# Log-sum-exp on one core: VectorE's aligned jump moved behind the last row's sum, and the two range checks cut differently

## The chip, the core and the metric

The kernel runs on one core of a Trainium2 chip. A core has five engines that take instructions from their own streams and meet through semaphores: TensorE (PE; its weight loads are shown as PEld), VectorE (DVE), ScalarE (ACT), GpSimd (POOL) and SyncE (SP), which here only issues transfers. Sixteen DMA engines carry the transfers between the device memory and the on-chip memory (SBUF, 128 partitions). The metric is the device time of one execution in microseconds (us), the median of several runs.

## The reference

```python
def setup_inputs():
    batch, seq, dim = 32, 512, 1024
    return {"x": np.random.randn(batch, seq, dim).astype(np.float32)}

def reference(x):
    max_x = np.max(x, axis=-1, keepdims=True)
    return (max_x.squeeze(-1) + np.log(np.sum(np.exp(x - max_x), axis=-1))).astype(np.float32)
```

For each of 16,384 rows of 1,024 numbers the logarithm of the sum of the exponentials is wanted: 67 MB are read and 64 KB written.

## The kernel before

**Fast way and slow way.** The kernel sums exp(x) without taking the maximum off. That is safe as long as every sum lies between `LOW` = 1e-15 and `HIGH` = 1e15. So it checks the sums, brings the verdict into one number (`count`, summed up by TensorE, then `fine` = 1 if it is below `HIGH`), and ScalarE and VectorE read `fine` and branch over a slow way that would compute everything again with the maximum. With this input the slow way is not taken.

**Tiling.** Each of the 128 partitions holds 128 rows, and one column of `sumexp` is the sum of one row per partition. The first `W` = 112 rows of a partition come in nine loads (`LOADS`), the last `B` = 16 rows in nine smaller pieces (`late`). All go through one ring of 48 rows in SBUF. SyncE issues the loads in order and waits only for ring space.

**The first 112 rows.** ScalarE takes the exponential in place (L226). For the operations named `R` VectorE sums whole rows (L237); for those named `F` GpSimd first adds the two halves of each row (L231) and VectorE sums the half rows (L190).

**The last 16 rows.** The pieces are cut across rows: columns 528 to 4288, then 12288 to 15776, then five pieces of 2656, 2000, 1456, 1088 and 800 columns up to column 12288, then the last 608 columns (`BACK`, the end of row 15), and last the first 528 columns (`HEAD`, the start of row 0). ScalarE takes the exponential of a piece (L280), and VectorE sums each row that is complete with an instruction that adds the two halves and accumulates (the helper `halves`, L199). It makes one instruction of the kind SCALAR_TENSOR_TENSOR and one DVE_READ_ACCUMULATOR that writes the column. Rows 0 and 15 are summed in two parts: `parts` holds the sums of the earlier parts; ScalarE writes the logarithm of each part's half, twice, next to the piece that is still to come (L310, tile `joins` in the ring), so that the exponential of the last pieces (L273 for row 15, L265 for row 0) adds the earlier part by its own accumulator. Row 15's sum goes to the last column of `sumexp`, row 0's to `last_sum` in PSUM.

**Checks.** `check_early` clamps `parts` and the 112 finished columns to the range and compares with the values (L159, L164); TensorE multiplies the result into `count` (L169). For each late row `add_up` lets TensorE add its column to `count` (L177), so that a sum too large shows there. A late check (L330) finds columns that are too small, over the 15 columns of rows 1 to 15. A last one (L340) looks at the largest input of the head piece, and TensorE's L345 closes `count`, from which VectorE makes `fine` (L347).

**Order and queues.** Nothing is scheduled by a planner: each engine runs what the code writes for it in that order, and a waiting instruction holds back all that stands behind it on its engine. `Counted.wait` writes a wait for another engine's count only when it is new. ScalarE's last work is the logarithm of 15 columns (L321), then that of row 0 (L323); then SyncE stores the last 16 columns of `res` (L325). The first 112 columns are stored before (L317). At its end SyncE waits for `done` from ScalarE and VectorE and for the early store, clears the semaphores (L406), and waits for the last store (L408).

**The aligned jump.** `addr_align(128, offset=0, max_nops=0)` in VectorE's stream puts the next instruction at the start of a block of 128 instructions; a branch jumps over the unused places. It stands before the sum of the last complete row (row 11, after the 800-column piece):

```python
        if k == len(late) - 3:
            nc.vector.addr_align(128, offset=0, max_nops=0)
        dve.wait(act, at)
```

Of the kernel before, what the change touches and what calls it, by code (L numbers as in the profile page):

```python
# [12 lines left out]
LOW, HIGH = 1e-15, 1e15  # L13
# [3 lines left out]
B = 16  # L17
# [39 lines left out]
def kernel(  # L57
# [5 lines left out]
    nc = tc.nc  # L63
# [4 lines left out]
    P = nc.NUM_PARTITIONS  # L68
    fp32 = mybir.dt.float32
    i32 = mybir.dt.int32  # L70
    AF = mybir.ActivationFunctionType
    AX = mybir.AxisListType
    ALU = mybir.AluOpType

    x_flat = x.flatten_outer_dims()
    n, d = x_flat.shape
    assert n % P == 0
    NC = n // P
    H = d // 2
    W = NC - B  # L80
# [6 lines left out]
    def source(e0, size):  # L87
        assert e0 >= W * d or e0 + size <= W * d
        return x_rest[:, e0 - W * d : e0 - W * d + size] if e0 >= W * d else x_rows[:, e0 : e0 + size]
# [8 lines left out]
    late = [(HEAD, start), (MID * d, B * d - BACK)]  # L98
# [2 lines left out]
        start += size  # L101
    late += [(B * d - BACK, B * d), (0, HEAD)]
    assert start == MID * d and sum(e - s for s, e in late) == B * d

    def sbuf(name, cols, dtype=fp32, rows=P):
        return nc.alloc_sbuf_tensor(name, [rows, cols], dtype).ap()

    ring = sbuf("ring", RING * d)
    sums_all = sbuf("sumexp", 2 + NC)
    parts, sumexp = sums_all[:, 0:2], sums_all[:, 2 : 2 + NC]  # L110
    res = sbuf("res", NC)
    clamped = sbuf("clamped", NC)
    bad = sbuf("bad", 3)
# [11 lines left out]
    act = Counted(nc, nc.scalar, "act")  # L125
    dve = Counted(nc, nc.vector, "dve")
# [16 lines left out]
    def load(i, here, done_before, size):  # L143
        for a, b, who, at in users:
            if a < here + size and b > here:
                sp.wait(who, at)
        users[:] = [u for u in users if not (u[0] < here + size and u[1] > here)]
        parts = [(0, FIRST), (FIRST, size)] if i == 0 else [(0, size)]
        return [
            nc.sync.dma_start(  # L150
                out=ring[:, here + a : here + b], in_=source(done_before + a, b - a)
            ).then_inc(landed[i], 16)
            for a, b in parts
        ]

    def check_early():
        n = 2 + W
        dve.wait(dve, dve.n)
        dve.did(nc.vector.tensor_scalar(  # L159
            out=clamped[:, 0:n], in0=sums_all[:, 0:n],  # L160
            scalar1=LOW, scalar2=HIGH, op0=ALU.max, op1=ALU.min,
        ))
        dve.wait(dve, dve.n)
        dve.did(nc.vector.scalar_tensor_tensor(  # L164
            out=clamped[:, 0:n], in0=clamped[:, 0:n], scalar=0.0, in1=sums_all[:, 0:n],
            op0=ALU.bypass, op1=ALU.not_equal, accum_out=bad[:, 0:1],
        ))
        pe.wait(dve, dve.n)
        pe.did(nc.tensor.matmul(count, lhsT=bad[:, 0:1], rhs=far, start=True, stop=False))  # L169
# [3 lines left out]
    def add_up():  # L173
        while sums:
            c, who, at = sums.pop(0)
            pe.wait(who, at)
            pe.did(nc.tensor.matmul(  # L177
                count, lhsT=ones, rhs=sumexp[:, c : c + 1], start=False, stop=False
            ))
# [3 lines left out]
    def reduce_folded():  # L183

        nonlocal early_sum
        while folded:
            c0, s0, p0, n0 = folded.pop(0)
            halves = ring[:, p0 : p0 + s0 * d].rearrange("p (c d) -> p c d", d=d)[:, :, 0:H]
            dve.wait(pool, n0)
            at = dve.did(nc.vector.reduce_sum(  # L190
                out=sumexp[:, c0 : c0 + s0], in_=halves, axis=AX.X
            ))
            users.append((p0, p0 + s0 * d, dve, at))
            if c0 < W:
                early_sum = at

    def halves(v, c):
        n = v.shape[1] // 2
        return dve.did(nc.vector.scalar_tensor_tensor(  # L199
            out=v[:, 0:n], in0=v[:, 0:n], scalar=1.0, in1=v[:, n : 2 * n],  # L200
            op0=ALU.mult, op1=ALU.add, accum_out=c,
        ))

    c = 0
# [5 lines left out]
    for i, (size, ops) in enumerate(loads):  # L210
# [11 lines left out]
        for k, (how, s) in enumerate(ops):  # L222
# [5 lines left out]
            if how == "F":  # L228
# [3 lines left out]
                    out=rows[:, :, 0:H], in0=rows[:, :, 0:H], in1=rows[:, :, H:d], op=ALU.add  # L232
# [15 lines left out]
    def place(e0):  # L248
        return e0 - MID * d + p if e0 >= MID * d else gap + GAP + e0

    joins = bass.AP(
        tensor=ring.tensor, offset=ring[:, gap : gap + 1].offset,
        ap=[ring.ap[0], [GAP - 2, 2], [1, 2]],
    )
    summed = set()
    seen = []
    for k, (s, e) in enumerate(late):
        i = len(loads) + k
        at0, at1 = place(s), place(s) + e - s
        [dma] = load(i, at0, W * d + s, e - s)  # L260
        act.wait(landed[i], 16)
        if k >= len(late) - 2:
            act.wait(act, joined)
        if k == len(late) - 1:
            head_sum = act.did(nc.scalar.activation(  # L265
                out=last_exp[:, 0 : e - s + 2], in_=ring[:, at0 - 2 : at1], func=AF.Exp,
                accum_out=last_sum,
            ))
            break
        if k == len(late) - 2:  # L270
            assert at1 == gap
            v = ring[:, at0 : at1 + 2]
            back_sum = act.did(nc.scalar.activation(  # L273
                out=v, in_=v, func=AF.Exp, accum_out=sumexp[:, NC - 1 : NC]
            ))
            sums.append((NC - 1, act, back_sum))
            add_up()
            continue
        v = ring[:, at0:at1]
        at = act.did(nc.scalar.activation(out=v, in_=v, func=AF.Exp))  # L280
        if k == 0:
            reduce_folded()
        if k == len(late) - 3:
            nc.vector.addr_align(128, offset=0, max_nops=0)
        dve.wait(act, at)
        seen.append((s, e))
        for r in range(1, B - 1):
            left = r * d
            for s0, e0 in sorted(seen):
                if s0 <= left < e0:  # L290
                    left = e0
            if r not in summed and left >= (r + 1) * d:
                summed.add(r)
                row = ring[:, place(r * d) : place(r * d) + d]
                sums.append((W + r, dve, halves(row, sumexp[:, W + r : W + r + 1])))
        if k == 0:
            halves(ring[:, at0 : place(0) + d], parts[:, 1:2])
        if k == 1:
            halves(ring[:, place((B - 1) * d) : at1], parts[:, 0:1])
            both = dve.n  # L300
            act.wait(dve, early_sum)
            ln_early = act.did(nc.scalar.activation(  # L302
                out=res[:, 0:W], in_=sumexp[:, 0:W], func=AF.Ln
            ))
            check_early()
        if k >= 1:
            add_up()
        if k == 2:
            act.wait(dve, both)
            joined = act.did(nc.scalar.activation(  # L310
                out=joins, in_=parts[:, :, None].to_broadcast([P, 2, 2]), func=AF.Ln, scale=0.5
            ))
    assert len(summed) == B - 2

# [1 line left out]
    sp.wait(landed[-2], 16)  # L316
    nc.sync.dma_start(out=out_rows, in_=res[:, 0:W]).then_inc(sp.sem, 16)  # L317

    act.wait(dve, dve.n)
    act.wait(act, back_sum)  # L320
    act.did(nc.scalar.activation(out=res[:, W + 1 : NC], in_=sumexp[:, W + 1 : NC], func=AF.Ln))  # L321
    act.wait(act, head_sum)
    act.did(nc.scalar.activation(out=res[:, W : W + 1], in_=last_sum, func=AF.Ln))  # L323
    sp.wait(act, act.n)
    nc.sync.dma_start(out=out_rest, in_=res[:, W:NC]).then_inc(stored, 16)  # L325


    dve.wait(dve, dve.n)
    dve.wait(act, back_sum)
    dve.did(nc.vector.scalar_tensor_tensor(  # L330
        out=clamped[:, W + 1 : NC], in0=sumexp[:, W + 1 : NC], scalar=LOW,
        in1=sumexp[:, W + 1 : NC], op0=ALU.max, op1=ALU.not_equal, accum_out=bad[:, 1:2],
    ))
    pe.wait(dve, dve.n)
    pe.did(nc.tensor.matmul(count, lhsT=bad[:, 1:2], rhs=far, start=False, stop=False))
    pe.wait(dve, less_at)
# [4 lines left out]
        out=over, in0=ring[:, at0 : at0 + half], scalar=CEILING,  # L341
        in1=ring[:, at0 + half : at1], op0=ALU.max, op1=ALU.max, accum_out=bad[:, 2:3],
# [15 lines left out]
    with nc.If(all_fine < 1):  # L358
# [5 lines left out]
        for c0 in range(0, NC, RING):  # L364
# [6 lines left out]
            for c1, c2 in ((c0, edge), (edge, c0 + s)):  # L371
                if c1 == c2:
                    continue
                nc.scalar.dma_start(
                    out=ring[:, (c1 - c0) * d : (c2 - c0) * d],
                    in_=source(c1 * d, (c2 - c1) * d),
# [4 lines left out]
                out=neg, in_=v, op=ALU.max, axis=AX.X, negate=True  # L381
# [3 lines left out]
                out=v, in0=v, in1=neg[:, :, None].to_broadcast([P, s, d])  # L385
# [5 lines left out]
                out=sumexp[:, c0 : c0 + s], in_=v, axis=AX.X  # L391
# [71 lines left out]
```

## Time and profile before

| what | value |
|---|---|
| median of 3 runs | 161.93 us (161.88 to 162.07) |
| profiled execution | 161.83 us |
| its span, first to last instruction | 160.1 us |
| VectorE busy | 114.2 us (71%) |
| ScalarE busy | 114.5 us (71%) |
| TensorE busy | 2.5 us (2%) |
| GpSimd busy | 37.3 us (23%) |
| mean transfer rate over the span | 420 GB/s |

The span is 1.7 us shorter than the execution's time; what lies around the span is not in the program. The busy shares are means over the whole span: the engines wait for loads early on, and are full only in the last 15 us. The chain of work that ended last is followed back by the profile from the last busy instruction; branches, semaphore instructions and the landing of a store are not busy work, so the chain does not hold what comes after 158.98 us.

### The profile page before, as it was taken

The page shows a single profiled execution, that of the slowest core. Times are in us where ns is not written, and L with a number is a line of the kernel's source. Part 1 is how long each engine was busy: PE and PEld are TensorE (multiplying, and loading weights), DVE is VectorE, ACT ScalarE, POOL GpSimd, SP SyncE. Part 2 cuts the span into 40 slices and gives each one's busy share as a digit, 9 for nine tenths or more (in the row PEclk, how much of TensorE's full clock was granted, in tenths as well). Part 3 has the DMA queues.
Part 4 walks back from the last instruction along what each step waited for, and adds up shares of the span by engine and source line. Part 5 has one row for each costly group of instructions (what it writes and reads, how often), then busy time and mean ns, then how long its engine had stood idle before and what let it go on. Part 6 is the DMA issues. An engine that isn't in the chain of part 4 may idle for free.

```text
span 160.1 us, 250 instructions
## 1 busy us (share of the span) xinstructions
PE 2.5 (2%) x38; PEld 1.3 (1%) x38; DVE 114.2 (71%) x60; ACT 114.5 (71%) x32; POOL 37.3 (23%) x11
## 2 busy tenths in 40 slices
PE   0000000000000000000000000000000000000033
PEld 0000000000000000000000000000000000000011
DVE  0000000019999499994999859959999999999986
ACT  3000059980799709995099949992999989799996
POOL 0000000000000000000000993690004979891000
DMA  8995996996996996997999999999999999999993
GB/s 319 507 507 254 507 524 262 524 524 262 524 524 262 524 524 262 524 475 311 483 442 442 442 426 409 409 409 472 405 396 454 458 409 393 421 437 425 414 402 114
DMA packets 3025, 67.18 MB, mean 420 GB/s; under 512 B 592, under 2 KB 592, under 8 KB 1488
## 3 DMA queue, kind: packets, MB, share of 16 engines
q1 hardware_dynamic: 3024, 67.18, 97.8%
q14 instruction: 1, 0.01, 0.0%
HBM read 67.11 MB, written 0.07 MB: 419 GB/s over the span
## 4 chain that ended last, share of the span: by engine, by line
DMA 51%; ACT 27%; DVE 20%; issue 0%; PE 0%
DMA ring<-in_x_dram 51%; ACT ring L226 19%; DVE sumexp L237 16%; ACT ring L280 7%; DVE sumexp L190 2%; DVE ring L199 2%; DVE over L340 0%; PE count L345 0%; ACT res L302 0%; DVE clamped L330 0%; DVE fine L347 0%; ACT ring L310 0%
## 5 line engine op out<-in xcount | busy, mean ns | idle before, releaser
L226 ACT ACTIVATE ring<-ring 128x16384 f32<-128x16384 f32 (+9 forms) x16 | 98.0, 6169 | 42.3 <-DMA ring<-in_x_dram 42.3
L237 DVE TENSOR_REDUCE sumexp<-ring 128x16 f32<-128x16384 f32 (+4 forms) x9 | 85.6, 9514 | 42.0 <-ACT ring L226 42.0
L231 POOL TENSOR_TENSOR ring<-ring 128x3072 f32<-128x3072 f32 (+3 forms) x7 | 37.1, 5314 | 107.1 <-ACT ring L226 107.1
L190 DVE TENSOR_REDUCE sumexp<-ring 128x6 f32<-128x3072 f32 (+3 forms) x7 | 18.4, 2659 | 0.0
L280 ACT ACTIVATE ring<-ring 128x3760 f32<-128x3760 f32 (+6 forms) x7 | 13.7, 2006 | 0.0
L199 DVE SCALAR_TENSOR_TENSOR ring<-ring 128x512 f32<-128x512 f32 (+2 forms) x16 | 9.6, 652 | 0.4 <-ACT ring L280 0.3
L135 ACT ACT_TABLE_LOAD x1 | 1.3, 1283 | 1.9 <-PEq L66 1.9
L169 PE MATMUL count<-far,bad 128*1 128x1 f32 x2 | 0.2, 164 | 152.6 <-DVE clamped L164 152.6
L177 PE MATMUL count<-sumexp,ones 128*1 128x1 f32 x30 | 2.0, 163 | 3.6 <-DVE ring L199 3.5
L136 DVE MEMSET ones<- 128x1 f32 x1 | 0.1, 59 | 2.0 <-PEq L66 2.0
L169 PEld LDWEIGHTS count<-far,bad 128*1 128x1 f32 x2 | 0.1, 82 | 152.6 <-DVE clamped L164 152.6
L199 DVE DVE_READ_ACCUMULATOR ring<-ring 128x1 f32 x16 | 1.4, 85 | 0.0
L177 PEld LDWEIGHTS count<-sumexp,ones 128*1 128x1 f32 x30 | 1.1, 81 | 4.5 <-DVE ring L199 4.5
L273 ACT ACTIVATE ring<-ring 128x610 f32<-128x610 f32 x1 | 0.7, 696 | 0.0
L265 ACT ACTIVATE last_exp<-ring 128x530 f32<-128x530 f32 x1 | 0.6, 595 | 0.0
L340 DVE SCALAR_TENSOR_TENSOR over<-ring 128x264 f32<-128x264 f32 x1 | 0.4, 428 | 0.0
L347 DVE TENSOR_SCALAR fine<-count 1x1 int32<-1x1 f32 x1 | 0.1, 146 | 0.3 <-PE count L345 0.3
L164 DVE SCALAR_TENSOR_TENSOR clamped<-clamped,sumexp 128x114 f32<-128x114 f32 x1 | 0.3, 279 | 0.0
L302 ACT ACTIVATE res<-sumexp 128x112 f32<-128x112 f32 x1 | 0.3, 278 | 0.0
L159 DVE TENSOR_SCALAR clamped<-sumexp 128x114 f32<-128x114 f32 x1 | 0.2, 221 | 0.0
L321 ACT ACTIVATE res<-sumexp 128x15 f32<-128x15 f32 x1 | 0.2, 203 | 0.0
L330 DVE SCALAR_TENSOR_TENSOR clamped<-sumexp 128x15 f32<-128x15 f32 x1 | 0.2, 174 | 0.0
(20 smaller groups left out, 2.3 us busy)
## 6 DMA issues: line engine op xcount, KB each, us to landing
ring<-in_x_dram SPq DMA_DIRECT2D x1, 7936.0 KB, 21.2
ring<-in_x_dram SPq DMA_DIRECT2D x1, 6912.0 KB, 23.9
ring<-in_x_dram SPq DMA_DIRECT2D x1, 6400.0 KB, 19.7
ring<-in_x_dram SPq DMA_DIRECT2D x1, 4608.0 KB, 15.9
ring<-in_x_dram SPq DMA_DIRECT2D x1, 3584.0 KB, 24.0
ring<-in_x_dram SPq DMA_DIRECT2D x1, 3072.0 KB, 19.1
ring<-in_x_dram SPq DMA_DIRECT2D x1, 1880.0 KB, 16.0
ring<-in_x_dram SPq DMA_DIRECT2D x1, 1744.0 KB, 19.8
```

The costliest lines, as they stand in the source:

```text
L135: nc.scalar.preload_act_table_set("natural_log_exp_and_others")
L169: pe.did(nc.tensor.matmul(count, lhsT=bad[:, 0:1], rhs=far, start=True, stop=False))
L177: pe.did(nc.tensor.matmul(count, lhsT=ones, rhs=sumexp[:, c : c + 1], start=False, stop=False))
L190: at = dve.did(nc.vector.reduce_sum(out=sumexp[:, c0 : c0 + s0], in_=halves, axis=AX.X))
L199: return dve.did(nc.vector.scalar_tensor_tensor(out=v[:, 0:n], in0=v[:, 0:n], scalar=1.0, in1=v[:, n : 2 * n], op0=ALU.mult, op1=ALU.add, ...
L226: at = act.did(nc.scalar.activation(out=v, in_=v, func=AF.Exp))
L231: at = pool.did(nc.gpsimd.tensor_tensor(out=rows[:, :, 0:H], in0=rows[:, :, 0:H], in1=rows[:, :, H:d], op=ALU.add))
L237: at = dve.did(nc.vector.reduce_sum(out=sumexp[:, c : c + s], in_=rows, axis=AX.X))
L265: head_sum = act.did(nc.scalar.activation(out=last_exp[:, 0 : e - s + 2], in_=ring[:, at0 - 2 : at1], func=AF.Exp, accum_out=last_sum,))
L273: back_sum = act.did(nc.scalar.activation(out=v, in_=v, func=AF.Exp, accum_out=sumexp[:, NC - 1 : NC]))
L280: at = act.did(nc.scalar.activation(out=v, in_=v, func=AF.Exp))
L340: dve.did(nc.vector.scalar_tensor_tensor(out=over, in0=ring[:, at0 : at0 + half], scalar=CEILING, in1=ring[:, at0 + half : at1], op0=ALU.m ...
```

## The change

Three things change. The sum of the first part of row 0 moves into `sumexp`'s own column of row 0, and the part of row 15 stands just ahead of the first column, so that one stretch of 1 + 112 + 4 = 117 columns holds both parts, the 112 early sums and the late rows 1 to 3. The early check runs over these 117 columns instead of 114; the late check over 12 columns (rows 4 to 15) instead of 15, and TensorE no longer adds the columns of rows 1 to 3 (`c < LATE`). The aligned jump moves from before the last row's sum to behind it. The late check is written ahead of ScalarE's late logarithm, which then waits for the check's count alone; it waited for the last row's sum and for row 15's sum.

```diff
+    LATE = W + late[0][1] // d
...
-    sums_all = sbuf("sumexp", 2 + NC)
-    parts, sumexp = sums_all[:, 0:2], sums_all[:, 2 : 2 + NC]
+    sums_all = sbuf("sumexp", 1 + NC)
+    sumexp = sums_all[:, 1 : 1 + NC]
+    part_15, part_0 = sums_all[:, 0:1], sumexp[:, W : W + 1]
+    parts = bass.AP(
+        tensor=sums_all.tensor, offset=sums_all.offset,
+        ap=[sums_all.ap[0], [1 + W, 2], [0, 2]],
+    )
...
     def check_early():
-        n = 2 + W
+        n = 1 + LATE
...
             c, who, at = sums.pop(0)
+            if c < LATE:
+                continue
...
-        if k == len(late) - 3:
-            nc.vector.addr_align(128, offset=0, max_nops=0)
         dve.wait(act, at)
...
+    nc.vector.addr_align(128, offset=0, max_nops=0)
+    dve.wait(dve, dve.n)
+    dve.wait(act, back_sum)
+    dve.did(nc.vector.scalar_tensor_tensor(
+        out=clamped[:, LATE:NC], in0=sumexp[:, LATE:NC], scalar=LOW,
+        in1=sumexp[:, LATE:NC], op0=ALU.max, op1=ALU.not_equal, accum_out=bad[:, 1:2],
+    ))
     act.wait(dve, dve.n)
-    act.wait(act, back_sum)
     act.did(nc.scalar.activation(out=res[:, W + 1 : NC], in_=sumexp[:, W + 1 : NC], func=AF.Ln))
     act.wait(act, head_sum)
...
-    dve.wait(dve, dve.n)
-    dve.wait(act, back_sum)
-    dve.did(nc.vector.scalar_tensor_tensor(
-        out=clamped[:, W + 1 : NC], in0=sumexp[:, W + 1 : NC], scalar=LOW,
-        in1=sumexp[:, W + 1 : NC], op0=ALU.max, op1=ALU.not_equal, accum_out=bad[:, 1:2],
-    ))
```

In the built program this is VectorE's end, by source line, operation, tiles (written, then read) and the semaphores that it waits for (`act`, `dve`, `pe` are counts of ScalarE, VectorE and TensorE; `landed17` is the last load's). ISA is the aligned jump. First before, then after:

```order
L199 SCALAR_TENSOR_TENSOR ring,sumexp<-ring 128x512
L199 SCALAR_TENSOR_TENSOR ring,sumexp<-ring 128x512 [waits act]
L284 ISA
L199 SCALAR_TENSOR_TENSOR ring,sumexp<-ring 128x512 [waits act]
L330 SCALAR_TENSOR_TENSOR clamped,bad<-sumexp 128x15 [waits act,dve]
L340 SCALAR_TENSOR_TENSOR over,bad<-ring 128x264 [waits landed17]
L347 TENSOR_SCALAR fine<-count 1x1 [waits pe]
```

And the same place after the change:

```order
L208 SCALAR_TENSOR_TENSOR ring,sumexp<-ring 128x512
L208 SCALAR_TENSOR_TENSOR ring,sumexp<-ring 128x512 [waits act] x2
L326 ISA
L329 SCALAR_TENSOR_TENSOR clamped,bad<-sumexp 128x12 [waits act,dve]
L346 SCALAR_TENSOR_TENSOR over,bad<-ring 128x264 [waits landed17]
L353 TENSOR_SCALAR fine<-count 1x1 [waits pe]
```

The jump has moved past one row's sum and now stands right ahead of the late check; the check itself and what follows keep their places and waits.

ScalarE's end before, from the last two plain exponentials to the reading of `fine`:

```order
L280 ACTIVATE ring<-ring 128x800 [waits landed15]
L273 ACTIVATE ring,sumexp<-ring 128x610 [waits act,landed16]
L265 ACTIVATE last_exp,last_sum<-ring 128x530 [waits landed17]
L321 ACTIVATE res<-sumexp 128x15 [waits act,dve]
L323 ACTIVATE res<-last_sum 128x1 [waits act]
L351 TENSOR_LOAD fine [waits dve]
```

And after:

```order
L289 ACTIVATE ring<-ring 128x800 [waits landed15]
L282 ACTIVATE ring,sumexp<-ring 128x610 [waits act,landed16]
L274 ACTIVATE last_exp,last_sum<-ring 128x530 [waits landed17]
L334 ACTIVATE res<-sumexp 128x15 [waits dve]
L336 ACTIVATE res<-last_sum 128x1 [waits act]
L357 TENSOR_LOAD fine [waits dve]
```

The order is the same; the late logarithm has one wait fewer, and the VectorE count it waits for is one instruction later, the late check's.

TensorE's stream before, whole:

```order
L458 UNCONDITIONAL_BRANCH [waits barrier_Pool_Activation_PE_DVE_SP_release]
L169 MATMUL count<-far,bad 1x1 [waits barrier_Pool_Activation_PE_DVE_SP_release,dve]
L177 MATMUL count<-sumexp,ones 1x1 x6
L177 MATMUL count<-sumexp,ones 1x1 [waits dve] x8
L177 MATMUL count<-sumexp,ones 1x1 [waits act]
L335 MATMUL count<-far,bad 1x1 [waits dve]
L337 MATMUL count<-steep,less 1x1
L345 MATMUL count<-steep,bad 1x1 [waits dve]
```

And after:

```order
L464 UNCONDITIONAL_BRANCH [waits barrier_Pool_Activation_PE_DVE_SP_release]
L176 MATMUL count<-far,bad 1x1 [waits barrier_Pool_Activation_PE_DVE_SP_release,dve]
L186 MATMUL count<-sumexp,ones 1x1 x3
L186 MATMUL count<-sumexp,ones 1x1 [waits dve] x8
L186 MATMUL count<-sumexp,ones 1x1 [waits act]
L341 MATMUL count<-far,bad 1x1 [waits dve]
L343 MATMUL count<-steep,less 1x1
L351 MATMUL count<-steep,bad 1x1 [waits dve]
```

Three column sums, those of rows 1 to 3, are gone from the stretch that needs no new wait.

More of the change, by code (lines that the diff above doesn't have):

```diff
@@ L296 @@
         if k == 0:
-            halves(ring[:, at0 : place(0) + d], parts[:, 1:2])
+            halves(ring[:, at0 : place(0) + d], part_0)
         if k == 1:
-            halves(ring[:, place((B - 1) * d) : at1], parts[:, 0:1])
+            halves(ring[:, place((B - 1) * d) : at1], part_15)
             both = dve.n
@@ L310 @@
             joined = act.did(nc.scalar.activation(
-                out=joins, in_=parts[:, :, None].to_broadcast([P, 2, 2]), func=AF.Ln, scale=0.5
+                out=joins, in_=parts, func=AF.Ln, scale=0.5
             ))
```

## The prediction

> **What bounds the kernel now.** I read the chain of work that ended last, then the order of time over the last 10 us, then what SyncE waited for, and last the DMA queues in short stretches of the end. The change touches nothing before the early check at 152 us, so only the end is worked through. The chain's last links (start, us, what):
>
> ```profile
> core 0 of [0], span 160.1 us
> ...
> 152.29 3.12 ACT ring L280 x2
> 155.42 0.02 issue
> 155.44 1.10 DVE ring L199 x3
> 156.54 0.13 issue
> 156.67 1.32 DVE ring L199 x5
> 157.99 0.02 issue
> 158.01 0.18 DVE clamped L330 x2
> ...
> 158.83 0.15 DVE fine L347
> ```
>
> By this chain VectorE's row sums would set the end. But it stops with the last busy instruction at 158.98, and the span runs to 160.1. The rows in order of time (start, us, engine, line) show a second chain beside it:
>
> ```profile
> 156.06 0.69 DVE L199 SCALAR_TENSOR_TENSOR ring<-ring 128x512 f32<-128x512 f32 x1
> ...
> 156.67 0.69 DVE L199 SCALAR_TENSOR_TENSOR ring<-ring 128x512 f32<-128x512 f32 x1
> ...
> 157.11 0.70 ACT L273 ACTIVATE ring<-ring 128x610 f32<-128x610 f32 x1
> ...
> 157.28 0.69 DVE L199 SCALAR_TENSOR_TENSOR ring<-ring 128x512 f32<-128x512 f32 x1
> ...
> 157.71 0.19 ACT L273 ACTIVATION_READ_ACCUMULATOR ring<-ring 128x1 f32 x1
> 157.81 0.59 ACT L265 ACTIVATE last_exp<-ring 128x530 f32<-128x530 f32 x1
> 157.90 0.08 DVE L199 DVE_READ_ACCUMULATOR ring<-ring 128x1 f32 x1
> 158.01 0.17 DVE L330 SCALAR_TENSOR_TENSOR clamped<-sumexp 128x15 f32<-128x15 f32 x1
> ...
> 158.12 0.08 DVE L330 DVE_READ_ACCUMULATOR clamped<-sumexp 128x1 f32 x1
> ...
> 158.39 0.20 ACT L321 ACTIVATE res<-sumexp 128x15 f32<-128x15 f32 x1
> ...
> 158.50 0.17 ACT L323 ACTIVATE res<-last_sum 128x1 f32<-128x1 f32 x1
> ...
> 158.69 0.34 SPq L325 DMA_DIRECT2D out_dram<-res  x1
> ```
>
> ScalarE goes without a gap through L273, L265, the late logarithm L321 (it starts at 158.39, as L265 ends at 157.81 + 0.59 = 158.40) and L323, and 0.02 us after that SyncE issues the last store. SyncE's own waits, and the stores' times from issue to landing (KB, us), tell which of the two chains is last:
>
> ```profile
> SPq L406 <- ACTq L403: 0.7, 1, 0.7
> ...
> SPq L408 <- SPq L408: 0.4, 1, 0.4
> ```
> ```profile
> out_dram<-res SPq DMA_DIRECT2D x1, 56.0 KB, 1.9
> ...
> out_dram<-res SPq DMA_DIRECT2D x1, 8.0 KB, 1.4
> ```
>
> L406 is released by the branches behind `fine`; after it SyncE waits 0.4 us more at L408, for the last store: 158.69 + 1.4 = 160.1, the end of the span. So the end is set by ScalarE and the store, and VectorE's check and verdict have about 0.4 us to spare.
>
> **The change part by part.** The sum goes against the profiled execution: span 160.1 plus 1.7 around it, 161.83, which is 0.1 below the median of 161.93.
>
> *Early check, 117 columns for 114.* The neighbours:
>
> ```profile
> 151.99 0.22 DVE L159 TENSOR_SCALAR clamped<-sumexp 128x114 f32<-128x114 f32 x1
> ...
> 152.25 0.28 DVE L164 SCALAR_TENSOR_TENSOR clamped<-clamped,sumexp 128x114 f32<-128x114 f32 x1
> ...
> 152.64 0.75 PE L177 MATMUL count<-sumexp,ones 128*1 128x1 f32 x14
> 153.06 0.08 DVE L199 DVE_READ_ACCUMULATOR ring<-ring 128x1 f32 x1
> ...
> 153.20 0.09 PEld L177 LDWEIGHTS count<-sumexp,ones 128*1 128x1 f32 x2 [0.23 <-DVE ring L199]
> ...
> 154.08 0.69 DVE L199 SCALAR_TENSOR_TENSOR ring<-ring 128x512 f32<-128x512 f32 x1 [0.33 <-ACT ring L280]
> ```
>
> From L164 (114 columns, 0.28) to L330 (15 columns, 0.17) a column costs 0.11 / 99 = 0.0011 us; three more on two instructions are 0.007 us. VectorE then stands idle for 0.33 us before 154.08, waiting for ScalarE: cost nothing, and 0.007 if that cover were gone. The late check gets three columns shorter, 0.003 us less. The part sums only change their place, with the same instructions and sizes; ScalarE's join reads them by another stride, which I put at nothing, since 4 columns go through it either way.
>
> *Three column sums fewer on TensorE.* They are six of the fourteen matmul rows in 0.75 us, so at most 0.3 us at 152.6, after which TensorE waits for VectorE anyway (0.23 at 153.20). No gain on the path.
>
> *The jump.* Its row before:
>
> ```profile
> L284 DVEq COMPARE_BRANCH  x1: 51/51/51, 156.5 to 156.5; - x1
> ```
>
> It ran at 156.5 for 51 ns on VectorE's sequencer while the engine was busy with the sum of 156.06. The sum behind it started at 157.28, 0.61 after its predecessor, as that did after the one of 156.06: the jump cost nothing. From its end (156.55) to 157.28 is 0.73, so with all that it loads it takes less than 0.73 us. After the change it can run when the last row's sum has been sent off, that is when ScalarE's 800 columns are done, 0.09 after 157.11, say at 157.25. Even 0.73 more is 157.98, and the check could not start before 158.01, since it waits for the last row's sum. Bounds for the check's delay: 0 and 0.02 (a branch that is sent one 51 ns step later); I take 0, nearest to the row of 157.28.
>
> *The late logarithm's wait.* The check is done at 158.12 + 0.08 = 158.20. From VectorE's accumulator read at 153.06 + 0.08 to TensorE's start at 153.20 it took 0.06 to pass a count on, so ScalarE could start at 158.26. It is not free until 158.39: 0.13 to spare. Queued behind the wait are L323, SyncE's store and ScalarE's reading of `fine`; all keep their times as long as that margin holds. The two delays above (0.02 and 0.007) do not use it up. The wait that goes was passed while L265 ran:
>
> ```profile
> L53 ACTq EVENT_SEMAPHORE  x2: 17/17/17, 156.3 to 157.9; - x2
> ```
>
> The second of these, 17 ns at 157.9, is the one removed: it lies within L265 (157.81 to 158.40), a gain between 0 and 0.017, and I take 0. What stays late next is L265 itself, behind the last loads.
>
> *A fetch of instructions beside the stores.* The queues from 157.30 to 157.95, in 40 slices of 0.016 us:
>
> ```profile
> DMA  0000000000000000000000900000000000000000
> GB/s 0 0 0 0 0 0 0 0 0 0 0 0 0 0 0 0 0 0 0 0 0 0 504 0 0 0 0 0 0 0 0 0 0 0 0 0 0 0 0 0
> ...
> q14 instruction: 1, 0.01, 5.1%
> ```
>
> One packet of instructions, the only one in the span, starts in slice 22, at 157.66, and takes 5.1% of 16 engines over 0.65 us, 0.53 us on one engine. If VectorE's jump asks for it (1.11 us earlier), it moves by as much as the jump, 0.75 us, to 158.4 to 158.95. The last store's packets come later:
>
> ```profile
> 158.41:159.50 1.09, 0.27 (x6) 0.09 (x2) 0.29 (x3) 0.26 (x3) 0.00 (x0) 1.00 0.00 0
> 159.53:159.75 0.22, 0.00 (x0) 0.00 (x0) 0.00 (x0) 0.00 (x0) 0.00 (x0) 1.00 0.42 37
> ```
>
> The DMA share (the last number but one) is zero from 158.41 to 159.50 and 0.42 from 159.53: the moved packet falls into an empty stretch. Cost 0; the bound above is in the first rival.
>
> *Sum:* -0.02 to +0.03, taken as 0: profiled about 161.83, median 161.93.
>
> *A rule and a row.* The Trainium skill, page "Runtime: NRT & Kernel Launch", section "Instruction fetch mechanics", says that a taken branch to a page which is not held stalls the engine until a transfer has brought that page. It speaks against this change, since the branch now stands right ahead of the check. The trace disagrees for the jump as it stands: the sum behind it ran at 157.28, ahead of the packet of 157.66. That page of the Trainium skill also has blocks of 16 KiB; 504 GB/s over 0.01625 us are 8 KB here. By the rule the sum would be the second rival's.
>
> **The rivals.**
>
> *First, slower: the packet meets the last store.* It decides if the packet starts after 159.0 (159.53 less 0.53). That would be so if TensorE's stream asks for it and not the jump: TensorE does one column sum every 0.61 us there, and with three fewer it reaches the same place in its stream 1.84 us later, so the packet would start at 157.66 + 1.84 = 159.50. For it speaks only that both engines were at work at 156.5. Against it: 1.11 us after the jump fits a request made there. Price: the 56 KB store, which had the packet beside it, took 1.9 to land, the 8 KB one 1.4, so up to 0.5; at 0.33 it is past the bound. 162.25 to 162.45.
>
> *Second, slower: the jump must wait for its block.* Two more places of the stream now stand ahead of the jump (the sum and its accumulator read). If that moves the next aligned place one block on, that block isn't held: asked for at 157.25, it starts to come 1.11 later and takes 0.53, 158.9. Then check (0.17 + 0.08) and 0.06: the logarithm at 159.2 for 158.39, 0.8 late; past 0.13 every microsecond goes to the end. 162.7.
>
> *Third, faster.* If the packet or the early jump held up the last loads or ScalarE in runs without a profile, moving it gives that back. The profile speaks against it: from 157.11 ScalarE has no gap at all, and the DMA slices are empty from 157.30 until the packet starts, so the loads' packets were through. To count, 0.33 would have to be found in a tail where I find 0.02. 161.5.
>
> **How the numbers follow.** 0.2% of 161.93 is 0.32 us, about what a measurement of this kernel can tell from no change: 161.61 to 162.25. No change on the path: 0.70, with its own range 161.8 to 162.1 by the spread of the runs before (161.88 to 162.07) and the terms' bounds. First rival 0.10, second 0.06, slower for a reason that I don't see 0.04: slower 0.20. Third rival with what I don't see: faster 0.10. The range of 161.65 to 162.35 holds the first case, the lower half of the first rival's price and the weaker form of the third.
>
> **What would show it.** Right: in the profile after, the branch at about 157.25, the late check at 158.01, the late logarithm L334 straight behind L274 at 158.4, the last store 0.3 later and landed after 1.4; the instruction packet 0.7 to 0.8 later than before, in the gap between the two stores. Wrong: ScalarE idle before L334 with VectorE named as the releaser; a late check that starts well after the last row's sum; an instruction packet within the last store, and that store's landing above 1.4; or a second instruction packet in the span.

## The result and the profile after

The changed kernel takes 161.71 us (median of 22 runs, 161.62 to 161.87), the kernel before, in as many runs beside it, 161.99 us (161.72 to 162.33). The ratio is 0.9985, with a 95% interval of 0.9979 to 0.9991: faster by 0.15%, a quarter of a microsecond (the two medians lie 0.28 us apart). That is inside the predicted range and inside the 0.2% which the prediction took for unmeasurable, but 22 runs a side do tell it from nothing, so "no change" was wrong.

The profiled execution after has a span of 160.3 us, no shorter than before. Its chain of work, last links (start, us, what):

```profile
core 0 of [0], span 160.3 us
...
152.43 3.14 ACT ring L289 x2
155.57 0.02 issue
155.60 2.55 DVE ring L208 x8
158.15 0.03 issue
158.18 0.18 DVE clamped L329 x2
...
158.99 0.15 DVE fine L353
```

All of it is 0.16 us later than before, from loads that landed later in this execution. Within the end, in order of time (start, us, engine, line):

```profile
157.28 0.70 ACT L282 ACTIVATE ring<-ring 128x610 f32<-128x610 f32 x1
...
157.97 0.59 ACT L274 ACTIVATE last_exp<-ring 128x530 f32<-128x530 f32 x1
158.05 0.08 DVE L208 DVE_READ_ACCUMULATOR ring<-ring 128x1 f32 x1
158.18 0.17 DVE L329 SCALAR_TENSOR_TENSOR clamped<-sumexp 128x12 f32<-128x12 f32 x1
...
158.56 0.20 ACT L334 ACTIVATE res<-sumexp 128x15 f32<-128x15 f32 x1
...
158.66 0.17 ACT L336 ACTIVATE res<-last_sum 128x1 f32<-128x1 f32 x1
...
158.85 0.34 SPq L338 DMA_DIRECT2D out_dram<-res  x1
```

Counted from the start of row 15's exponential (157.11 before, 157.28 after), the check starts at 0.90 both times, the late logarithm at 1.28, the last store at 1.58 before and 1.57 after. SyncE's last waits and the stores' landing:

```profile
SPq L412 <- ACTq L409: 0.7, 1, 0.7
...
SPq L414 <- SPq L414: 0.4, 1, 0.4
```
```profile
out_dram<-res SPq DMA_DIRECT2D x1, 56.0 KB, 1.6
...
out_dram<-res SPq DMA_DIRECT2D x1, 8.0 KB, 1.4
```

The aligned jump's row after, and the transfers from 158.30 to 159.50 in 40 slices of 0.03 us:

```profile
L326 DVEq COMPARE_BRANCH  x1: 51/51/51, 157.4 to 157.4; - x1
```
```profile
GB/s 299 225 209 135 90 15 0 0 0 273 0 0 0 0 0 0 0 0 0 0 0 0 0 0 0 0 0 0 0 0 0 0 0 0 0 0 0 0 0 0
...
q14 instruction: 1, 0.01, 2.0%
```

The packet of instructions is now in slice 9, at 158.57: behind the early store's data and ahead of the last store's.

So the profile after shows the end that the prediction described, and no gain in it. The gain is in a number that is in no row: an execution's time less its span. For the profiled executions it is 161.83 - 160.14 = 1.69 us before and 161.87 - 160.30 = 1.57 after; over all 22 runs after it is 1.49 on average, with a mean span of 160.23. I call it the part outside the span. The experiments give it for the kernel before too: 1.69 to 1.70 us on average over 21 to 33 runs a time, with a mean span of 160.20 to 160.23. Against these the span has not moved, and the part outside is 0.21 us shorter. The 22 runs of the kernel before that stand beside the change have no spans on record; whether the rest of the 0.28 us between the two medians is more than scatter is not shown.

### The profile page after: what moved, and what is told of

Same layout as the page of the kernel before. It is cut to its first block, busy times and chain, and to the rows that moved or that the text cites. A ratio compares the mean times of both kernels' runs of the same rounds, so it can differ in the third digit from the quotient of the medians.

```text
span 160.3 us, 237 instructions
## 1 busy us (share of the span) xinstructions
PE 2.3 (1%) x32; PEld 1.2 (1%) x32; DVE 114.2 (71%) x60; ACT 114.5 (71%) x32; POOL 37.3 (23%) x11
## 4 chain that ended last, share of the span: by engine, by line
DMA 51%; ACT 27%; DVE 20%; issue 0%; PE 0%
DMA ring<-in_x_dram 51%; ACT ring L235 19%; DVE sumexp L246 16%; ACT ring L289 7%; DVE sumexp L199 2%; DVE ring L208 2%; DVE over L346 0%; PE count L351 0%; ACT res L309 0%; DVE clamped L329 0%; DVE fine L353 0%; ACT ring L317 0%
## 5 line engine op out<-in xcount | busy, mean ns | idle before, releaser
L274 ACT ACTIVATE last_exp<-ring 128x530 f32<-128x530 f32 x1 | 0.6, 593 | 0.0
```

Source lines behind the costliest of these rows:

```text
L274: head_sum = act.did(nc.scalar.activation(out=last_exp[:, 0 : e - s + 2], in_=ring[:, at0 - 2 : at1], func=AF.Exp, accum_out=last_sum,))
```

## The experiments

Each time stands beside runs of the kernel before on the same chip; "outside" is the mean over a kernel's runs of its time less its span (one run scatters by 0.02 to 0.05 us, and spans are on record to 0.1 us). The ratio is that to the kernel before in the same set of runs; in the row "after" that one had 161.99 us. e4 has five runs, the others ten or more. Instructions of ScalarE are counted in the built program, against the kernel before.

| run | what | ScalarE's instructions | median us | ratio, 95% interval | mean span | outside |
|---|---|---|---|---|---|---|
| before | | 0 | 161.90 to 161.92 | | 160.2 | 1.69 to 1.70 |
| after | the change | -1 | 161.71 | 0.9985 [0.9979, 0.9991] | 160.23 | 1.49 |
| e1 | jump alone | 0 | 161.92 | 1.0004 [0.9995, 1.0013] | 160.23 | 1.71 |
| e2 | wait alone | -1 | 161.76 | 0.9988 [0.9979, 0.9997] | 160.20 | 1.54 |
| e3 | columns alone | 0 | 161.89 | 1.0005 [0.9996, 1.0014] | 160.22 | 1.72 |
| e4 | no jump | 0 | 162.42 | 1.0036 [1.0022, 1.005] | 160.76 | 1.70 |
| e5 | after, one more that runs | 0 | 161.85 | 0.9998 [0.9988, 1.0008] | 160.19 | 1.73 |
| e6 | before, one less, not run | -1 | 161.71 | 0.9987 [0.9978, 0.9997] | 160.22 | 1.50 |
| e7 | after, one more, not run | 0 | 161.86 | 0.9998 [0.9988, 1.0007] | 160.18 | 1.70 |
| e8 | after, one less, not run | -2 | 161.51 | 0.9973 [0.9964, 0.9983] | 160.19 | 1.32 |
| e9 | after, two less | -3 | 161.53 | 0.998 [0.9971, 0.9989] | 160.26 | 1.34 |
| e10 | after, many less, not run | -10 | 161.61 | 0.9979 [0.9969, 0.9988] | 160.25 | 1.35 |
| e11 | before, one more, not run | +1 | 161.74 | 0.9988 [0.9979, 0.9997] | 160.20 | 1.53 |
| e12 | before, four more, not run | +4 | 161.83 | 0.9995 [0.9986, 1.0005] | 160.29 | 1.52 |
| e13 | after, ScalarE aligned early | jump | 161.97 | 1.0 [0.9991, 1.0009] | 160.63 | 1.34 |
| e14 | e13, one more, not run | jump | 161.97 | 1.0005 [0.9996, 1.0014] | 160.67 | 1.33 |
| e15 | before, ScalarE aligned early | jump | 161.87 | 0.9998 [0.9989, 1.0008] | 160.62 | 1.34 |
| e16 | after, ScalarE aligned late | jump | 161.56 | 0.9979 [0.997, 0.9988] | 160.19 | 1.37 |
| e17 | before, ScalarE aligned late | jump | 161.59 | 0.9982 [0.9972, 0.9991] | 160.31 | 1.35 |

### The parts one by one: e1, e2, e3

The jump alone:

```diff
-        if k == len(late) - 3:
-            nc.vector.addr_align(128, offset=0, max_nops=0)
...
+    nc.vector.addr_align(128, offset=0, max_nops=0)
     dve.wait(dve, dve.n)
     dve.wait(act, back_sum)
```

> Only the aligned jump is moved behind the last row's sum; checks, waits and column layout are those of the kernel before. Theory A (the jump and its instruction packet held something up in many executions, outside what one profile shows): this kernel alone gives most of the gain, 0.2 to 0.28 us less than before, and its instruction packet starts 0.7 to 0.9 us later, near 158.5. Theory B (the shorter TensorE and ScalarE streams, or the wait, give the gain): within 0.08 us of before. Theory C (the prediction: nothing on the path): also within 0.08 us of before.

The wait alone (the late check, over its old 15 columns, is written ahead of the logarithm):

```diff
+    dve.wait(dve, dve.n)
+    dve.wait(act, back_sum)
+    dve.did(nc.vector.scalar_tensor_tensor(
+        out=clamped[:, W + 1 : NC], in0=sumexp[:, W + 1 : NC], scalar=LOW,
+        in1=sumexp[:, W + 1 : NC], op0=ALU.max, op1=ALU.not_equal, accum_out=bad[:, 1:2],
+    ))
     act.wait(dve, dve.n)
-    act.wait(act, back_sum)
```

> Only the late check is written ahead of the late logarithm, which then waits for the check's count alone; jump and columns as before. Theory A: no gain, within 0.08 us of before. Theory B in the form that ScalarE's removed wait gives it: 0.15 us or more less than before. The prediction: within 0.02 us, the logarithm starting straight behind row 0's exponential.

The columns alone are the change's diff without its two other parts: 117 and 12 columns, three TensorE sums fewer.

> Only the columns are recut: early check over 117 columns, late check over 12, three TensorE column sums fewer; jump and wait as before. Theory A: no gain, within 0.08 us of before. Theory B in the form that TensorE's shorter stream gives it: 0.15 to 0.28 us less than before, and in the part outside the span (1.7 us before, 1.5 after).

The wait alone gives the gain (161.76, 1.54 outside); jump and columns give none (161.92 and 161.89). The instruction packet of e1, in 40 slices of 0.016 us from 158.20 to 158.85:

```profile
GB/s 303 248 303 222 221 221 165 166 83 83 0 28 0 0 0 0 0 0 0 504 0 0 0 0 0 0 0 0 0 0 0 0 0 0 0 0 0 0 0 0
...
q14 instruction: 1, 0.01, 3.7%
```

It starts in slice 19, at 158.51. That of e3, from 157.30 to 157.95:

```profile
GB/s 0 0 0 0 0 0 0 0 0 0 0 0 0 0 0 0 0 0 0 0 0 0 0 504 0 0 0 0 0 0 0 0 0 0 0 0 0 0 0 0
...
q14 instruction: 1, 0.01, 4.5%
```

Slice 23, 157.67, as before the change, although TensorE's stream is three sums shorter here. So the packet follows VectorE's jump and not TensorE.

### No jump at all: e4

```diff
-        if k == len(late) - 3:
-            nc.vector.addr_align(128, offset=0, max_nops=0)
```

> The kernel before without any aligned jump. Theory A: if the jump's place is what costs, taking it away changes the time by 0.2 us or more, faster if the packet alone was the harm, slower if VectorE then crosses into its next block at a worse place. The profile shows whether the instruction packet at 157.7 is the jump's: without the jump it should be gone from the span or start elsewhere; if it stays at 157.7 it is another engine's. Theory B: within 0.08 us of before, packet unmoved if it is TensorE's.

Slower by 0.36%, and this time in the span. In order of time:

```profile
158.03 0.17 DVE L328 SCALAR_TENSOR_TENSOR clamped<-sumexp 128x15 f32<-128x15 f32 x1
...
158.49 0.08 DVE L328 DVE_READ_ACCUMULATOR clamped<-sumexp 128x1 f32 x1 [0.29 <-issue]
...
158.71 0.34 SPq L323 DMA_DIRECT2D out_dram<-res  x1
```

Its transfers from 158.50 to 160.90, in 40 slices of 0.06 us, and the last store's landing:

```profile
GB/s 0 0 0 0 0 0 0 0 0 0 0 0 0 0 0 137 0 19 54 41 18 5 0 0 0 0 0 0 0 0 0 0 0 0 0 0 0 0 0 0
...
q14 instruction: 1, 0.01, 0.8%
```
```profile
out_dram<-res SPq DMA_DIRECT2D x1, 8.0 KB, 2.1
```

Between the check and its own accumulator read, which begins 0.1 us after the check in all the other profiles, VectorE stands for 0.29 us for nothing that the profile shows. I read this as the edge of VectorE's instruction block. Then the packet starts in slice 15 (159.4), just ahead of the last store's data, and that store takes 2.1 us to land instead of 1.4: 158.71 + 2.1 = 160.8, the end of the span. This is the first rival's price, 0.7 us in the profile and 0.5 in the medians. That the packet is the cause is inferred: the store's data rows end at 159.8, hardly later than before, and what keeps the landing back after that is in no row. The early store speaks for it. It lands after 1.9 to 2.1 us in the seven profiles in which VectorE's jump stands ahead of the last row's sum and ScalarE has no late jump, so that the packet comes ahead of the store's data, and after 1.6 us in the nine in which VectorE's jump stands behind that sum and the packet comes later. VectorE's standstill makes the verdict late too: SyncE begins its last wait at about 160.2 here and at 159.7 before, so by these figures the standstill alone would have cost about 0.1 us. If it is the edge of a block, only the check stands between it and the jump of the changed kernel.

### The length of ScalarE's stream: e5 to e8

The wait that the change removes is one instruction of ScalarE, 17 ns within L265's time. e2 cuts nothing else, so either the wait itself or the length of the stream is at work. e5 keeps the new wait and puts one instruction back, far ahead:

```diff
+        if i == 3:
+            nc.scalar.wait_ge(landed[0], 16)
         act.wait(landed[i], 16 * len(dma))
```

> The changed kernel with one instruction more in ScalarE's stream, far from the end: a second wait, long satisfied, ahead of an exponential at about 75 us, so that ScalarE's stream is as long as before the change, while the late logarithm still waits for the check alone. Theory L (the length of ScalarE's stream sets 0.2 us of the part outside the span): time back at that of before, 161.9, and 1.7 us outside the span. Theory S (what the late logarithm waits for gives the gain): as the changed kernel, 161.7, and 1.5 us outside the span. Both: span as before within 0.1.

e6 shortens ScalarE's stream in the kernel before by an instruction of the slow way, which is not taken, and puts it on VectorE (e8 does the same to the changed kernel):

```diff
     with nc.If(all_fine < 1):
-        nc.scalar.wait_ge(sp.sem, 16)
+        nc.vector.wait_ge(sp.sem, 16)
         nc.scalar.wait_ge(stored, 16)
```

> The kernel before, with ScalarE's stream shortened by one instruction that never runs: in the slow way, which this input does not take, the wait for the early store stands on VectorE instead of ScalarE. Nothing that runs is changed. Theory L: 0.15 to 0.25 us faster than before, 1.5 us outside the span. Theory S: as before, 161.9, 1.7 us outside.

e7 lengthens the changed kernel there:

```diff
     with nc.If(all_fine < 1):
+        nc.scalar.wait_ge(landed[0], 16)
+        nc.scalar.wait_ge(landed[1], 16)
         nc.scalar.wait_ge(sp.sem, 16)
```

> The changed kernel with ScalarE's stream lengthened by one instruction that never runs (a second wait in the slow way). Theory L: the gain is gone, 161.9 and 1.7 us outside the span. Theory S: 161.7 and 1.5 us outside. If e5 loses the gain and this keeps it, it is the number of instructions that run, not the length of the stream.

> The changed kernel with ScalarE's stream one instruction shorter still, by the same move in the slow way as in the run on the kernel before. Theory L as a step (an end of a block of instructions that the stream passes or not): no more to gain, 161.7 and 1.5 us outside. Theory L as a slope (each instruction costs): another 0.2 us, 161.5 and 1.3 us outside. Theory S: 161.7.

Theory L holds in all four. One more instruction of ScalarE, run or not, takes the gain away (1.73 and 1.70 outside); one less, never run, gives it to the kernel before (1.50), and a second one gives the changed kernel as much again (1.32, 161.51 us). What the logarithm waits for has no part in it. Nor do the lengths of other streams show one: e6, with one VectorE instruction more, has 1.50 where e2, without it, has 1.54; e3, with three of TensorE fewer, has 1.72; e4, with one of VectorE fewer, 1.70. e5 and e7 change ScalarE's stream alone. e8 looked like a slope of 0.19 us per instruction.

### How far it goes: e9 to e12

e9 is e8 with ScalarE's share of the program's end moved:

```diff
-        if read.ins.engine == mybir.EngineType.DVE:
+        if read.ins.engine == mybir.EngineType.Activation:
             read.then_inc(done, 1)
...
-        nc.scalar.wait_ge(again, rows + 32)
+        nc.vector.wait_ge(again, rows + 32)
...
-    nc.scalar.sem_inc(done, 1)
+    nc.vector.sem_inc(done, 1)
```

> The changed kernel with ScalarE's stream two instructions shorter, by moving work to VectorE and nothing else: the wait for the early store in the slow way, and the signal that ends the program (ScalarE gives its part of it with its reading of the verdict, VectorE at its end). Three fewer than before the change in all. If each instruction of ScalarE's stream costs 0.19 us outside the span, as the last four runs suggest: 1.70 - 3 x 0.19 = 1.13 us outside, 161.33 in all. If the gain ends after two: 1.32 outside, 161.5. Span 160.2 in both.

(In e9 VectorE's stream is two instructions longer than before, in e10 four shorter.) e10 is e9 with `for c0 in range(0, RING, RING)` in the slow way and without its two stores:

> As the run with two fewer, and the slow way, which does not run, is cut to its first third, and its two stores and the last third's loads are left out with it: ten ScalarE instructions fewer than before the change. Shows where the gain ends. On a slope without end: 1.70 - 10 x 0.19 is below zero, so it must end; if it ends at an edge close by, 1.0 to 1.3 us outside and 161.2 to 161.5 in all. If moving an edge brings a new one, the time can also rise.

e11 and e12 are the kernel before with two and with eight waits more in the slow way, which make one and four instructions:

> The kernel before with one ScalarE instruction more that never runs. On the slope: 1.89 us outside the span, 162.1. If the kernel before already stands at the top of the step: 1.70 and 161.9.

> The kernel before with four ScalarE instructions more that never run. On the slope: 1.70 + 4 x 0.19 = 2.46 us outside, 162.7. At the top of a step: 1.70 and 161.9, as with one more.

The slope fell: 1.35, 1.34, 1.32, 1.49 to 1.54, 1.70 to 1.73, 1.53, 1.52 us for -10, -3, -2, -1, 0, +1 and +4 instructions. It is a step with a peak, and the kernel before stood on the peak: one instruction more (e11, of ScalarE alone) would have helped it nearly as much as one less (161.74 and 161.71). In e12 a second packet of instructions is to be seen, behind the span. From 160.30 to 162.00, in slices of 0.043 us:

```profile
GB/s 0 0 0 0 0 0 0 0 0 0 0 0 0 0 0 0 0 0 0 0 0 0 0 0 0 0 0 0 0 0 193 0 0 0 0 0 0 0 0 0
...
q14 instruction: 1, 0.01, 1.7%
```

In the profile before, the same stretch of time holds no packet at all, and no other profile has one behind its span, not even e11's, with one instruction more. So this packet does not mark the peak: e12, which has it, stands at 1.52, and the kernel before, which has none, at 1.70.

### An aligned jump for ScalarE: e13 to e17

If an edge of an instruction block lies among what ScalarE runs behind the program, a jump to the start of a block takes the length out of it.

```diff
+        if i == 3:
+            nc.scalar.addr_align(128, offset=0, max_nops=0)
         act.wait(landed[i], 16 * len(dma))
```

> The changed kernel with an aligned jump in ScalarE's stream too, ahead of the exponential of the fourth load (about 70 us), so that everything behind it, to the end of the program and past it, stands at a set place in a block. Theory E (what costs is an edge of a block that falls on ScalarE's instructions behind the end of the program; the kernel before has its length at the worst place): 1.35 us outside the span or less, 161.5 to 161.6. Theory G (any change of the length shifts the part outside by chance, no edge): no reason for less than the changed kernel's 1.49. Against both: a jump that itself costs would lengthen the span beyond 160.2.

> As the run with ScalarE's aligned jump, and one ScalarE instruction more that never runs, the one that took the whole gain from the changed kernel (1.49 to 1.70 us outside). Theory E: no edge is near any more, so the part outside is the same within 0.05 us of the run without it. Theory G: it moves by 0.1 to 0.2 us.

> The kernel before with ScalarE's aligned jump alone, ahead of the fourth load's exponential; its two waits before the late logarithm stay. Theory E: the same part outside as the changed kernel with that jump, within 0.05 us, so the change's whole gain and more is had without the change. Theory G: 1.5 to 1.7 us outside.

The figures are those of theory E: 1.34, 1.33 and 1.34 us outside. That they come from an edge, and that it lies behind the program, they do not show. The instruction that cost 0.21 us without the jump costs nothing with it, and the kernel before comes to the same figure as the changed one. But the span grew by 0.4 us. The chain of work of e13, and below it of the kernel before, at the same load:

```profile
72.24 24.43 DMA ring<-in_x_dram
```
```profile
72.19 23.87 DMA ring<-in_x_dram
```

The load on which the chain stands took 0.56 us longer. It took 24.38 to 24.59 us in the three runs with this jump and 23.87 to 23.91 in the sixteen others. ScalarE's jump ran at 60.5, and one packet of instructions came among the loads, in the stretch from 64.0 to 65.5:

```profile
q1 hardware_dynamic: 16, 1.05, 162.7%
q14 instruction: 1, 0.01, 1.3%
```

The packet starts at 64.7, 4.2 us after the jump. So the place of ScalarE's jump matters as that of VectorE's does. e16 and e17 put it ahead of row 0's exponential, when the loads' packets are through:

```diff
+        if k == len(late) - 1:
+            nc.scalar.addr_align(128, offset=0, max_nops=0)
         act.wait(landed[i], 16)
```

> The changed kernel with ScalarE's aligned jump at its end, ahead of row 0's exponential (the last load's), so that the packet of instructions which the jump asks for comes after the last load's packets and before the last store's, near 158.4. If the early jump lost 0.4 us of span to its packet among the loads, the span is back at 160.2 and the part outside stays at 1.33: 161.55, faster than before by 0.2%. If the span stays at 160.6, the jump or the longer program itself cost it, and it is 161.95.

> The kernel before with the same jump of ScalarE ahead of row 0's exponential and nothing else. Theory E: the same 161.55 and 1.33 us outside the span, without any part of the change. If the change holds a gain of its own, this stays above the run on the changed kernel by 0.1 us or more.

The span is back at 160.19 and the part outside stays at 1.37: 161.56 us. In e16's profile two packets of instructions now lie between the loads and the last store, from 157.30 to 159.50 in slices of 0.055 us:

```profile
GB/s 0 38 0 0 0 0 0 0 0 0 0 0 0 0 0 8 138 244 393 228 98 17 0 0 149 0 0 0 8 24 16 16 0 0 0 0 0 0 0 0
...
q14 instruction: 2, 0.02, 2.7%
```
```profile
out_dram<-res SPq DMA_DIRECT2D x1, 56.0 KB, 2.3
...
out_dram<-res SPq DMA_DIRECT2D x1, 8.0 KB, 1.4
```

They make the early store land after 2.3 us, which costs nothing, and leave the last one at 1.4. The kernel before with that jump (e17, 161.59) is as fast as the changed one with it. With ScalarE's jump in both kernels, the change has no gain of its own that these runs can tell. Both, and e8 at 161.51, are faster than the kernel before. Their medians are below that of the changed kernel too, but they did not run beside it, and their intervals overlap its own.

## Why the prediction was right or wrong

- **What bounds the end: right.** Row 15's and row 0's exponentials, the two logarithms and the last store end last, before and after; the 0.4 us wait of SyncE's last instruction is there in both profiles.
- **Early check, fewer sums: right.** e3 alone, 161.89 beside 161.90.
- **The jump: right in the span.** It ran at 157.4, where 157.25 plus this execution's 0.16 puts it, the check followed the last sum at once, and e1 alone is at 161.92. The packet moved by 0.9 us, 0.75 of it relative to ScalarE, into the empty stretch, as worked out.
- **The late logarithm's wait: wrong in its size, and the step that failed.** The prediction costed the removed instruction by its own 17 ns and its place under L265: "a gain between 0 and 0.017, and I take 0". On ScalarE's path in the span that holds: the logarithm starts straight behind L274. But e2, which does this part alone, measured 0.16 us outside the span, e6 0.20 by an instruction that never runs, and the change 0.21. Behind it stands a second step, the sum itself: "span 160.1 plus 1.7 around it" took the part outside as given. It is the term that moved, from 1.70 to 1.49. What lies around the span has no row in the program, but its length depends on the program.
- **The third rival (faster) came true in sign, not in mechanism.** It looked for a hold-up by the packet or the jump in other executions and had 0.10. e1 denies that; nothing in the prediction looked at the length of a stream.
- **The first rival's mechanism did not act here, but e4 supports it:** a packet just ahead of the last store's data, with the standstill before it, costs 0.5 us. The idea that TensorE owns the packet fell with e3.
- **The second rival did not come.** Behind the jump the check starts 0.05 us after the last sum's end, as against 0.03 before. No jump in these runs shows the stall that the Trainium skill's page "Runtime: NRT & Kernel Launch", section "Instruction fetch mechanics", gives to a branch to a page not held; whether the pages were held is in no row. The same section of the Trainium skill says that passing into the next page in order is mostly hidden: e4's 0.29 us of standing still is against that, if it is the edge of a block, as I read it.
- **The chances.** By its own bound of 0.2% the result, 0.15%, lies with "no change", the case that had 0.70. But the sum was taken as 0, and the gain is clear of noise. That the range held it is luck as far as the mechanism goes: no term of the prediction stands for it.

Not shown: what the time outside the span is spent on. The experiments tie it to the number of ScalarE's instructions. That an edge of ScalarE's blocks costs 0.2 to 0.4 us there (1.52 or 1.70 less 1.33) is inferred from the levels and from the aligned jump's taking the dependence away. The traces do not bear it out behind the program. They hold no instruction there, but semaphore events: the last one comes 1.46 us after the end of the span in the profiles before, after and of e8 alike, whose executions have 1.69, 1.57 and 1.33 us outside (e11's comes after 1.60, with 1.53 outside). The events of the last 0.4 us ahead of the span do not move either. Where the time is spent, and why the values beside the peak are 1.5 on both sides and lower only further down, stays open.

## What to carry to other kernels

Add up the time outside the span as a term of its own, and compare it between versions before looking for a few tenths of a microsecond in the rows. In this kernel the number of instructions in ScalarE's stream, also of those that never run, mattered more than what they do; a version that gains by one instruction fewer may only have left an unlucky length, and one instruction more elsewhere in the stream is the cheap test. An aligned jump in ScalarE's stream held the part outside at 1.33 to 1.37 us here, but it brings a packet of instructions later (1.1 us after VectorE's late jumps, 4.2 us after ScalarE's among the loads): try it where that packet meets neither a load that the chain stands on nor the last store.

## What the runs showed of the hardware that was not expected

- One instruction of ScalarE more or less, run or not, moved an execution by 0.16 to 0.24 us at an unlucky length, all outside the span (e2, e5 to e7, e11); at two to ten instructions fewer the part outside lay flat at 1.32 to 1.35 us.
- With one packet of 8 KB of instructions (504 GB/s in a slice of 0.016 us in e1 and e3) among the loads, the load that the chain stood on took 0.5 to 0.7 us longer (e13 to e15); with one just ahead of the last 8 KB store's data, that store landed after 2.1 us instead of 1.4 (e4).
- Without the aligned jump VectorE stood for 0.29 us between an instruction and its own accumulator read (e4).
